# Merge gates in block products over three walks, second half normalised by way of DRAM, SSM data in fewer DMAs

## The chip, the cores and the metric

The kernel runs on one core of one Trainium2 chip. Its engines work side by side: TensorE (PE in the profile; its weight loads are PEld), VectorE (DVE), ScalarE (ACT), GpSimd (POOL) and SyncE (SP), which here issues DMAs only. The metric is the device time of one execution in microseconds. Before the change it is 2546.79 us, the median of three runs from 2544.15 to 2549.72.

## What is computed

A decoder layer on x of 1024 positions by 2048 channels, all in float32:

```
h = rms_norm(x, norm_w)
q, k, v, a_gate, u, z, g_a, g_s = split(h @ w_in)       # 1024,256,256,1024,1024,1024,2048,2048 columns
q, k = rms_norm per head of 64
y_a = (window-128 attention with sinks(q, k, v) * silu(a_gate)) @ w_attn_proj
y   = gelu(diagonal complex SSM(u))                     # 64 groups of 16 channels, 64 states each
glu_a, glu_b = split(y @ w_glu + b_glu)
y_s = (glu_a * sigmoid(glu_b) * silu(z)) @ w_ssm_proj
out = x + (sigmoid(g_a) * y_a + sigmoid(g_s) * y_s) @ w_out
```

## The kernel before

Activations lie transposed: channels on the 128 partitions, positions along the row, in two halves of 512 positions (h = 0 and 1). A float32 operand is split in two float32r tiles, hi (a cast on ScalarE) and lo (the rest, a subtraction on VectorE; `split`, L80), and a product of a 128x128 weight block with a 128x512 operand takes three matmuls: hi*hi, hi*lo, lo*hi. `proj` (L110) makes one output tile of 128 columns for one half: two weight tiles of 128x1024 (8 blocks of 128x128 each), each loaded by SyncE (`load_w`, L99: tag raw, two tiles; tags whi and wlo, two each), split, and followed by 16 hi and 8 lo matmuls; it yields behind each of the two. So an output tile of the input projection costs 48 matmuls.

The stages follow one another in the code: u and z of half 0 beside the preparation of the SSM (`ssm_prep`), k, v, q of half 0 (`kvq`), then half 1 (`build_raw(1)`, u, k, v, q) beside the attention of half 0, z and eight merge-gate tiles of half 1 beside the attention of half 1, then the other gates beside the SSM (`ssm`, L660): eight merge-gate tiles of w_in 36 to 51 (g_a), the attention gate (28 to 35) and 16 tiles of 52 to 67 (g_s) of half 1, and after `build_raw(0)`, which loads and splits x of half 0 again, the same gates of half 0. The gates' tiles go to DRAM (GD, GSD, AGD). Operands are x times norm_w alone; rstd of each position is multiplied onto the output (`sigmoids` L171, `gate` L180, `evac` L278, `uproj` L195).

The GLU and the two branch projections (`four`, L881) and the output projection (`out1` to `out3`) already use a scheme of seven block products for a 2x2 by 2x2 product: sums of weight tiles are made on GpSimd (`wadd`, L854, into tiles of tag ws), sums of operands by `combos` (L811), and the seven operands are loaded and split by `load_ops` (L779). `out2` (L1055) is the one closest to the change: for each j it loads three weight tiles (`rring`), makes two sums, two splits (`wsplit`, with a third whi/wlo pair from pool cb in `wring`) and two block products of 24 matmuls, 6 and 5.

The SSM reads its coefficients (PWD, L687, eight DMAs for each tile of eight groups), its kernel matrix (KD, L744, eight DMAs for a tile) and writes its result (YD, L760, 16 DMAs for a tile) on SyncE's queue; px (L703) and py (L752, L753) are its matmuls, bm and ct the tables that GpSimd makes for them (tt, L665).

What runs when is decided at build time. Side work is a generator that `drive` pulls at a given rate for each step of the main one (`spawn`, L1122); a scheduler then puts the instructions of each engine in one fixed order by priority (weights are lifted by `high_priority`), and takes tile buffers from the pools as they come free. On the chip each engine goes through its order and waits at each instruction for what it needs.

## Time and profile before

| | us |
|---|---|
| median of three runs | 2546.79 |
| the profiled execution | 2542.53 |
| its span, first to last instruction | 2540.8 |
| TensorE busy | 2459.2 (97%) |
| VectorE busy | 1557.5 (61%) |
| ScalarE busy | 963.8 (38%) |
| GpSimd busy | 921.5 (36%) |
| mean granted clock of TensorE | 0.988 of 2.4 GHz |

The rows further down come from this one execution. Busy TensorE time is the union of overlapping matmuls, so the rate of matmuls is read from where they start. A row of DMA issues counts the issues of one line and says how long after its issue a transfer has landed.

### The profile page before, as it was taken

The numbers are of one execution on the slowest core, as the hardware profiler recorded it, in microseconds if no ns is written. First come the engines' busy times: TensorE is split into PE (matmuls) and PEld (weight loads), VectorE is DVE, ScalarE is ACT, GpSimd is POOL, SyncE is SP. The second block draws the span as 40 slices with busy tenths as digits, with TensorE's granted clock in tenths as the row PEclk, the third lists the DMA queues.
The fourth block names the chain that finished last, engine by engine and source line by source line (L and its number), as shares of the span: only waits on it lengthen the run. The fifth ranks groups of instructions, "written<-read, shape, count | busy, mean of one in ns | idle before, by whom it ended". The sixth has DMA issues, their size and how long they took to land. (4 is left out here: it accounts for less than half of the span.)

```text
span 2540.8 us, 30817 instructions
## 1 busy us (share of the span) xinstructions
PE 2459.2 (97%) x11012; PEld 2007.1 (79%) x11012; DVE 1557.5 (61%) x2040; ACT 963.8 (38%) x1492; POOL 921.5 (36%) x715
## 2 busy tenths in 40 slices
PE   7999999999999999999999999999999999899998
PEld 5878878788878878888788788887878877678886
DVE  7995566894686455736573432236587687745543
ACT  5333454463666433434442222224352331333311
POOL 5101004341453434251412300014547466414576
PEclk9999999999999999999999999999999999999999
DMA  6544343323223456565757743336368676888675
GB/s 212 177 135 133 92 141 104 96 72 99 96 92 121 141 161 165 177 166 142 206 159 240 259 164 124 120 120 216 108 223 296 203 252 227 266 298 278 222 234 176
DMA packets 217306, 438.95 MB, mean 173 GB/s; under 512 B 63521, under 2 KB 75841, under 8 KB 217153
## 3 DMA queue, kind: packets, MB, share of 16 engines
q1 hardware_dynamic: 181376, 344.34, 44.4%
q0 software_dynamic: 19504, 63.28, 6.6%
q10 hardware_dynamic: 16272, 29.38, 3.0%
q8 instruction: 86, 1.41, 0.2%
q14 instruction: 68, 0.55, 0.1%
HBM read 341.93 MB, written 94.96 MB: 172 GB/s over the span
## 5 line engine op out<-in xcount | busy, mean ns | idle before, releaser
L121 PE MATMUL ps<-hh,whi 128*128 128x512 f32 x2144 | 845.3, 395 | 4.7 <-ACT whi L81 4.7
L122 PE MATMUL ps<-hl,whi 128*128 128x512 f32 x2144 | 842.1, 393 | 1.0 <-DVE hl L144 1.0
L82 DVE TENSOR_TENSOR wlo<-wraw,whi 128x1024 fp32r<-128x1024 f32 (+1 forms) x344 | 445.2, 1295 | 488.9 <-PE ps L125 247.7
L81 ACT CAST whi<-wraw 128x1024 fp32r<-128x1024 f32 (+1 forms) x344 | 349.8, 1018 | 637.2 <-PE ps L122 372.0
L125 PE MATMUL ps<-hh,wlo 128*128 128x512 f32 x2144 | 542.0, 391 | 1.7 <-DVE wlo L82 1.7
L121 PEld LDWEIGHTS ps<-hh,whi 128*128 128x128 f32 x2144 | 405.1, 189 | 93.8 <-ACT whi L81 6.4
L122 PEld LDWEIGHTS ps<-hl,whi 128*128 128x128 f32 x2144 | 405.3, 189 | 86.7 <-DVE hl L144 2.1
L125 PEld LDWEIGHTS ps<-hh,wlo 128*128 128x128 f32 x2144 | 401.5, 188 | 86.9 <-DVE wlo L82 2.1
L81 ACT CAST whi<-ws 128x1024 fp32r<-128x1024 f32 x80 | 84.2, 1054 | 292.5 <-POOL ws L855 80.4
L82 DVE TENSOR_TENSOR wlo<-ws,whi 128x1024 fp32r<-128x1024 f32 x80 | 116.4, 1456 | 115.7 <-ACT whi L81 74.4
L855 POOL TENSOR_TENSOR ws<-wraw 128x512 f32<-128x512 f32 (+1 forms) x72 | 135.0, 1875 | 132.9 <-DVE wlo L82 95.8
L421 POOL TENSOR_TENSOR pa<-ph,c_mct 128x512 fp32r<-128x512 f32 x32 | 43.7, 1364 | 253.3 <-ACT ph L81 253.2
L178 POOL DMA_DIRECT2D gsd<-sg x32 | 17.8, 556 | 226.7 <-ACT sg L177 214.8
L177 ACT ACTIVATE sg<-sg 128x512 f32<-128x512 f32 x64 | 40.6, 634 | 136.5 <-DVE sg L176 136.4
L402 ACT ACTIVATE scs<-scs,m,rq 128x128 f32<-128x128 f32 x128 | 62.2, 487 | 61.9 <-DVE m L396 61.8
L1000 POOL TENSOR_TENSOR mt<-mt,pa 128x512 f32<-128x512 f32 x32 | 56.3, 1762 | 74.9 <-DMA sgs<-gsd 22.6
L178 POOL DMA_DIRECT2D gd<-sg x32 | 17.7, 555 | 177.7 <-ACT sg L177 165.3
L861 PE MATMUL psm<-q1h,whi 128*128 128x512 f32 x160 | 64.7, 405 | 6.8 <-ACT whi L81 6.8
L861 PE MATMUL psm<-q4h,whi 128*128 128x512 f32 x160 | 66.2, 414 | 3.0 <-DVE mt L995 3.0
L862 PE MATMUL psm<-q4l,whi 128*128 128x512 f32 x160 | 65.6, 410 | 1.4 <-DVE q4l L82 1.4
L861 PE MATMUL psm<-q2h,whi 128*128 128x512 f32 x160 | 62.7, 393 | 2.7 <-ACT qa L892 2.6
L862 PE MATMUL psn<-q3l,whi 128*128 128x512 f32 x160 | 62.8, 393 | 1.6 <-DVE q3l L82 1.6
(352 smaller groups left out, 4165.7 us busy)
## 6 DMA issues: line engine op xcount, KB each, us to landing
wraw<-w_in SPq DMA_DIRECT2D x268, 512.0 KB, 3.6
wraw<-w_out SPq DMA_DIRECT2D x72, 512.0 KB, 5.2
x<-xT SPq DMA_DIRECT2D x96, 256.0 KB, 3.9
gd<-sg POOLq DMA_DIRECT2D x32, 256.0 KB, 3.7
gsd<-sg POOLq DMA_DIRECT2D x32, 256.0 KB, 2.9
wraw<-w_glu SPq DMA_DIRECT2D x16, 512.0 KB, 4.2
wraw<-w_attn SPq DMA_DIRECT2D x16, 512.0 KB, 4.7
sga<-gd SPq DMA_DIRECT2D x32, 256.0 KB, 4.4
```

What stands on the lines that cost most here:

```text
L81: S.copy(hi, src)
L82: V.tensor_tensor(lo, src if src2 is None else src2, hi.bitcast(F32), op=ALU.subtract)
L121: PE.matmul(ps, hi[:, kk, :], rh[kt], start=(kt == 0), stop=False)
L122: PE.matmul(ps, hi[:, kk, :], rl[kt], start=False, stop=False)
L125: PE.matmul(ps, lo[:, kk, :], rh[kt], start=False, stop=(kt == last))
L177: S.activation(sg, sg, AF.Sigmoid)
L402: S.activation(sc[:, r, :], sc[:, r, :], AF.Exp, bias=m4[:, r:r + 1], scale=RQ[h, p][:, b, 2 * r + e:2 * r + e + 1], accum_out=den[:, r:r ...
L421: G.tensor_tensor(a, ph.bitcast(F32), mb, op=ALU.mult)
L855: G.tensor_tensor(o, a, b, op=ADD)
L861: PE.matmul(ps, hi[:, c0 + k, :], rh, start=(first and k == 0), stop=False, skip_group_check=True)
L862: PE.matmul(ps, hi[:, c0 + k, :], rl, start=False, stop=False, skip_group_check=True)
L1000: G.tensor_tensor(t, t, p, op=ADD)
```

## The change

The 32 merge-gate tiles of the two halves are no longer made one by one. They form 16 pairs (a tile j and the tile j + 8 of the same gate); a pair is a 2x2 product, two output tiles and two halves of positions over two halves of channels, and is made with seven block products instead of eight, in three walks over the pairs:

- `gates1`: products 1 and 2 with the plain operands of half 1 give one of the four outputs; product 1 is kept in DRAM (QG[0]).
- `gates2`: three weight tiles, two sums on GpSimd in place (in the raw tiles), products 6 and 5; two intermediate results go to DRAM (QG[1], QG[2]).
- `gates3`: four weight tiles, three sums, products 7, 4 and 3, which give the other three outputs.

`inputs` makes the operand sums (HD) and the normalised operands of half 1 (HN), from x blocks loaded through GpSimd's queue, while k, v, q and the attention gate of half 0 are made; `build_n` reads half 1 back from HN, so that no rstd is multiplied onto the outputs of half 1. `build_raw(0)` is gone. Attention gates are plain tiles: of half 0 ahead of the attention (kept in AT and multiplied onto it in `combos`), of half 1 beside the SSM. The SSM's coefficients are written 16 times over in DRAM and read in one DMA, its matrix is first laid out in DRAM (TZD) and read in one DMA, its result is written in two DMAs by ScalarE's queue; YD's layout and the order of w_glu's rows follow. Weights have three raw tiles in pool w, and one instead of two in pool cb, which exists from the seventh pair of the third walk on; pool g has 8 buffers and holds operands 6 and 7, pool g2 four more.

```diff
+RAW = 3
...
-    YD = dp.tile([2, NG * 16, 8, 64], F32, name="yd")
-    PWD = dp.tile([2, 8, NG, 64], F32, name="pwd")
+    YD = dp.tile([2, 8, 128, 8, 64], F32, name="yd")
+    PWD = dp.tile([2, 8, 16, NG, 64], F32, name="pwd")
...
-        raw = wp.tile([128, KC, 128], F32, tag="raw", name="wraw")
+        raw = wp.tile([128, KC, 128], F32, tag="raw", bufs=RAW, name="wraw")
...
-    def build_raw(h):
+    def build_n():
...
-            x = load_x(kt, h, tag="ld" if kt % 2 else "x")
+            x = sp.tile([128, TH], F32, tag="ld" if kt % 2 else "x", bufs=3 if kt % 2 else 2, name="hn")
+            nc.sync.dma_start(x, HN[kt])
...
     def evac(ps, out, h):
-        V.tensor_tensor(out, ps, rstd[h], op=ALU.mult)
+        if h:
+            S.copy(out, ps)
+        else:
+            V.tensor_tensor(out, ps, rstd[h], op=ALU.mult)
...
-                    for j in range(8):
-                        nc.sync.dma_start(w[n][16 * j:16 * j + 16],
-                                          PWD[n, 7 - j, g0:g0 + 8, :].unsqueeze(0).to_broadcast([16, 8, 64]))
+                    nc.sync.dma_start(w[n], PWD[n, :, :, g0:g0 + 8, :].rearrange("j h g p -> (j h) g p"))
...
-                for j in range(8):
-                    nc.sync.dma_start(tz[16 * j:16 * j + 16],
-                                      KD[:, gs + q * 8:gs + q * 8 + 8, 128 - 16 * j:256 - 16 * j])
+                nc.sync.dma_start(tz, TZD[:, gs + q * 8:gs + q * 8 + 8, :])
...
-                for i in range(8):
-                    for s in range(2):
-                        nc.sync.dma_start(YD[s, g0 * 16:(g0 + 8) * 16, i, :].rearrange("(g h) c -> h g c", h=16),
-                                          yt[16 * i:16 * i + 16, :, 64 * s:64 * s + 64])
+                for s in range(2):
+                    nc.scalar.dma_start(YD[s, 2 * bt + q], yt[:, :, 64 * s:64 * s + 64])
...
+        for k in range(8):
+            b12, b11 = block(k, 0, "x"), block(k, 1, "x")
+            nc.gpsimd.dma_start(HN[k], b11)
+            G.tensor_tensor(b11, b11, b12, op=SUB)
+            nc.gpsimd.dma_start(HD[0, k], b11)
+            yield
...
+    def gates1(ops, a, b):
+        for p in range(a, b):
+            kind, _, na, nb, ia, ib = PAIRS[p]
+            with tc.high_priority(offset=200):
+                t1 = wsplit(rring(wq(na, 0)))
+            x = bank(0)
+            product(x, t1, 0, ops[1])
+            q = et("qa")
+            S.copy(q, x)
+            nc.gpsimd.dma_start(QG[0][p], q)
+            yield
...
+            product(x, t2, 0, ops[2], first=False)
+            gate(kind, ia, 1, x)
+            yield
+
+    def gates2(ops, a, b):
+        for p in range(a, b):
+            kind, _, na, nb, ia, ib = PAIRS[p]
+            q = ld(QG[0][p], "qa")
+            with tc.high_priority(offset=200):
+                w5, r, w6 = rring(wq(nb, 0)), rring(wq(nb, 1)), rring(wq(na, 0))
+                wadd(w5, w5, r)
+                wadd(w6, w6, w5)
+                t = wsplit(w6)
+            y = bank(0)
+            product(y, t, 0, ops[6])
+            v = et("qb")
+            V.tensor_tensor(v, q, y, op=SUB)
+            nc.gpsimd.dma_start(QG[1][p], v)
+            yield
+            with tc.high_priority(offset=200):
+                t = wsplit(w5)
+            y = bank(0)
+            product(y, t, 0, ops[5])
+            e = et("qe")
+            V.tensor_tensor(e, y, v, op=ADD)
+            nc.gpsimd.dma_start(QG[2][p], e)
+            yield
...
+                    w[7], r, w[4], w[3] = rring(wq(na, 0)), rring(wq(nb, 0)), rring(wq(nb, 1)), rring(wq(na, 1))
+                    wadd(w[7], w[7], r)
...
+                    wadd(w[3], w[3], w[4])
+                    wadd(w[3], w[3], w[7])
+                    t = wsplit(w[3])
+                y = bank(1 if p > 5 else 0)
+                product(y, t, 0, ops[3])
+                gate(kind, ia, 0, y, ADD, e)
...
+            product(z, t, 0, ops[7])
+            gate(kind, ib, 0, z, SUB, e)
...
+            product(z, t, 0, ops[4], first=False)
+            gate(kind, ib, 1, z, SUB, v)
...
-    spawn(ssm(bp, pp), 0.8)
-    drive(sigmoids(36, GD[1], hh, hl, rstd[1], 8, 16))
-    drive(gate(28, AGD[1], hh, hl, rstd[1], AOD[1]))
-    drive(sigmoids(52, GSD[1], hh, hl, rstd[1], 0, 16))
-    hh, hl = build_raw(0)
-    drive(gate(28, AGD[0], hh, hl, rstd[0], AOD[0]))
-    drive(sigmoids(36, GD[0], hh, hl, rstd[0], 0, 16))
+    spawn(ssm(bp, pp), 1.1)
+    drive(plain("o", 28, 1, hh, hl))
+    drive(gates1(og, 8, 12))
+    operands((6,), 1.5)
+    drive(gates1(og, 12, 15))
...
+    operands((3,), 1.5)
+    drive(gates2(og, 0, 15))
+    drain2()
+    operands((7, 4), 4.0)
+    drive(gates2(og, 15, 16))
+    drain2()
+    drive(gates3(og, 0, 6))
     drain()
```

Where the order of instructions moves, at the places that the prediction speaks of:

GpSimd beside the SSM, before (the gate tiles of half 1; bm, bmu, ct and ctu are the SSM's tables, the DMAs the gate tiles):

```order
L665 TENSOR_TENSOR ct<-c_9116,p_8212 128x1152
L665 TENSOR_TENSOR ct<-ct,ctu 128x1152
L665 TENSOR_TENSOR ctu<-c_9945,p_9196 128x1152
L178 DMA gsd_81<-sg 128x512 x2
L665 TENSOR_TENSOR bm<-pwr,bre 128x8x64
L665 TENSOR_TENSOR bm<-pwr,bim 128x8x64
L665 TENSOR_TENSOR ct<-c_9944,p_9195 128x1152
L665 TENSOR_TENSOR bm<-bm,bmu 128x8x64
L665 TENSOR_TENSOR ct<-ct,ctu 128x1152
L665 TENSOR_TENSOR bmu<-pwi,bre 128x512
L665 TENSOR_TENSOR ctu<-c_10065,p_9196 128x1152
```

GpSimd beside the SSM in the second walk, after (L849 are the weight sums, L1199 and L1207 the DMAs of QG; the pair's second sum stands three rows further down, behind a bm and another L1199):

```order
L849 TENSOR_TENSOR wraw<-wraw 128x1024
L645 TENSOR_TENSOR bm<-pwr,bre 128x8x64
L645 TENSOR_TENSOR bm<-pwr,bim 128x8x64
L645 TENSOR_TENSOR ct<-c_10215,p_9529 128x1152
L645 TENSOR_TENSOR bm<-bm,bmu 128x8x64
L1199 DMA qg_96<-qb 128x512
L645 TENSOR_TENSOR ct<-ct,ctu 128x1152
L645 TENSOR_TENSOR bmu<-pwi,bre 128x512
L1207 DMA qg_97<-qe 128x512
L645 TENSOR_TENSOR ctu<-c_10292,p_9530 128x1152
L849 TENSOR_TENSOR wraw<-wraw 128x1024
```

The SSM's operations were alone with the gates' DMAs and stand now between weight sums on which a product waits.

SyncE in the second pass of the output projection, before, with what each issue waits for (the numbers tell tiles apart; DMAHW are earlier DMAs):

```order
L843 DMA wraw_18842<-w_out 128x1024 [waits DMAHW6_49,Pool_49]
L843 DMA wraw_18844<-w_out 128x1024 [waits DMAHW7_49,Pool_49]
L843 DMA wraw_18846<-w_out 128x1024 [waits DMAHW0_49]
L878 DMA qa_18840<-qd0_92 128x512 [waits DMAHW2_49,DVE_49]
L843 DMA wraw_18942<-w_out 128x1024 [waits DMAHW3_49,Pool_49]
L843 DMA wraw_18944<-w_out 128x1024 [waits DMAHW6_49,DMAHW5_49,Pool_49]
L843 DMA wraw_18946<-w_out 128x1024 [waits DMAHW7_49]
L878 DMA qa_18940<-qd0_92 128x512 [waits DMAHW0_49,DVE_49]
```

SyncE in the second walk, after:

```order
L837 DMA wraw_10906<-w_in 128x1024 [waits DMAHW7_49,DMAHW1_49,Pool_49]
L872 DMA qa_11021<-qg0_95 128x512 [waits DMASW3_49,DVE_49]
L837 DMA wraw_10908<-w_in 128x1024 [waits DMAHW3_49,DVE_49]
L837 DMA wraw_10910<-w_in 128x1024 [waits DMAHW4_49,DVE_49]
L837 DMA wraw_11023<-w_in 128x1024 [waits DMAHW5_49,DMAHW3_49,Pool_49]
L872 DMA qa_11129<-qg0_95 128x512 [waits DMAHW6_49,DMASW5_49,DVE_49]
L837 DMA wraw_11025<-w_in 128x1024 [waits DVE_49]
L837 DMA wraw_11027<-w_in 128x1024 [waits DMAHW0_49,DVE_49]
L837 DMA wraw_11131<-w_in 128x1024 [waits DMAHW7_49,DMAHW1_49,Pool_49]
```

A raw tile was free as soon as GpSimd had added it; now the second and third load of a pair wait for VectorE, which splits the sums out of the raw tiles.

## Rows read from the trace of the kernel before

**Rows 1.** Page, part 1: busy us (share of the span) and instructions of each engine.

```profile
PE 2459.2 (97%) x11012; PEld 2007.1 (79%) x11012; DVE 1557.5 (61%) x2040; ACT 963.8 (38%) x1492; POOL 921.5 (36%) x715
```

**Rows 2.** Windows: stretch, its us, busy PE PEld DVE ACT POOL, PEclk, DMA, GB/s.

```profile
1420.00:1710.00 290.00, 289.11 (x1262) 238.55 (x1263) 96.22 (x100) 80.75 (x95) 31.62 (x43) 0.99 0.46 152
1710.00:1745.00 35.00, 30.53 (x120) 21.38 (x120) 22.56 (x27) 14.40 (x23) 15.57 (x17) 1.00 0.77 249
...
2045.00:2225.00 180.00, 161.08 (x656) 126.62 (x655) 136.42 (x146) 45.25 (x61) 104.88 (x64) 0.95 0.74 244
...
2316.00:2403.00 87.00, 87.00 (x385) 72.03 (x385) 40.96 (x44) 21.95 (x27) 42.23 (x17) 1.00 0.78 260
```

**Rows 3.** Timeline of PE, second pass of the output projection: start us, us, instruction.

```profile
2331.01 0.39 PE L861 MATMUL psn<-q6h,whi 128*128 128x512 f32 x1
...
2336.45 0.39 PE L861 MATMUL psn<-q5h,whi 128*128 128x512 f32 x1
...
2352.77 0.39 PE L861 MATMUL psn<-q6h,whi 128*128 128x512 f32 x1
...
```

**Rows 4.** Lines by form, GpSimd: x count | busy us, mean ns | idle before.

```profile
L855 POOL TENSOR_TENSOR ws<-wraw 128x1024 f32<-128x1024 f32 x24 | 60.0, 2499 | 57.0 <-DVE wlo L82 27.5 <-DMA wraw<-w_out 10.3 <-DMA x<-xT 5.0
...
L665 POOL TENSOR_TENSOR bm<-bm,bmu 128x512 f32<-128x512 f32 x16 | 26.4, 1650 | 0.3
...
L665 POOL TENSOR_TENSOR ct<-ct,ctu 128x1152 f32<-128x1152 f32 x8 | 24.6, 3073 | 0.3
...
L665 POOL TENSOR_TENSOR ctu<-c,p 128x1152 f32<-128x1152 f32 x8 | 21.2, 2652 | 0.2
...
L178 POOL DMA_DIRECT2D gsd<-sg x32 | 17.8, 556 | 226.7 <-ACT sg L177 214.8 <-ACT X L735 8.6 <-DMA pwi<-pwd 3.3
...
```

**Rows 5.** Timeline of GpSimd in the SSM; last row: PE's px, lines by form.

```profile
890.99 2.27 POOL L665 TENSOR_TENSOR ctu<-c,p 128x1152 f32<-128x1152 f32 x1
893.22 1.29 POOL L665 TENSOR_TENSOR bm<-bm,bmu 128x512 f32<-128x512 f32 x1
...
895.06 2.68 POOL L665 TENSOR_TENSOR ct<-ct,ctu 128x1152 f32<-128x1152 f32 x1
...
L703 PE MATMUL px<-uq,bm 128*128 128x128 f32 x128 | 18.5, 306 | 9.3 <-POOL bm L665 9.3
```

**Rows 6.** DMA issues of SSM data: x count, KB each, median us to landing.

```profile
tz<-kd SPq DMA_DIRECT2D x64, 64.0 KB, 3.5
...
yd<-yt SPq DMA_DIRECT2D x128, 32.0 KB, 2.7
...
pwr<-pwd SPq DMA_DIRECT2D x64, 32.0 KB, 2.1
...
```

**Rows 7.** Timeline of the output projection's second pass: sums, splits, casts, an issue.

```profile
2327.97 3.31 POOL L855 TENSOR_TENSOR ws<-wraw 128x1024 f32<-128x1024 f32 x1 [4.97 <-DMA x<-xT]
...
2334.86 1.23 DVE L82 TENSOR_TENSOR wlo<-ws,whi 128x1024 fp32r<-128x1024 f32 x1 [5.24 <-ACT whi L81]
...
2339.78 2.39 POOL L855 TENSOR_TENSOR ws<-wraw,ws 128x1024 f32<-128x1024 f32 x1 [1.21 <-DVE wlo L82]
...
2342.20 1.06 ACT L81 CAST whi<-ws 128x1024 fp32r<-128x1024 f32 x1 [4.00 <-POOL ws L855]
...
2351.38 0.33 SPq L843 DMA_DIRECT2D wraw<-w_out  x1
```

**Rows 8.** DMA issues of weights, with median us to landing.

```profile
wraw<-w_in SPq DMA_DIRECT2D x268, 512.0 KB, 3.6
wraw<-w_out SPq DMA_DIRECT2D x72, 512.0 KB, 5.2
```

**Rows 9.** Waits of GpSimd: combos behind VectorE; us in total, times, longest.

```profile
POOL cb_b L820 <- DVE cb_d L819: 48.3, 11, 10.2
```

**Rows 10.** Lines by form: a split of operand tiles on VectorE.

```profile
L82 DVE TENSOR_TENSOR q7l<-op,q7h 128x512 fp32r<-128x512 f32 x20 | 18.9, 996 | 5.8 <-ACT q7h L81 5.6
```

**Rows 11.** Tile ws (sums of weights): ns at least, in the middle, at most.

```profile
L82 DVE TENSOR_TENSOR wlo<-ws,whi x80: 1207/1225/3981, 1706.2 to 2513.9; 128x1024 fp32r<-128x1024 f32 x80
```

241 lines of the change are left out of this document (168 added, 73 removed).

## Prediction

> **What bounds the kernel now.** I read the shares of the engines first: TensorE is busy in 2459.2 of 2540.8 us [rows 1], so the kernel can gain in two ways only, fewer matmuls or fewer of the 82 us in which TensorE stands. Next come the stretches [rows 2]. The one that the change rewrites most (gate projections, 1420 to 1710) has TensorE busy in 289.11 of 290 us at a granted clock of 0.99: no wait is left to win there. TensorE stands elsewhere, 4.5 us at the start of the GLU (1710 to 1745) and 19 us in the last branch product (2045 to 2225). The rate of TensorE is read off a timeline [rows 3]: 24 matmuls start between 2331.01 and 2336.45 us, so a block product of 24 takes 5.44 us and a matmul 0.2267 us.
>
> **What the change takes off TensorE.** The order of instructions has 10,050 matmuls of 128x512 before and 9,666 after: the 32 merge-gate tiles in two halves cost 32 x 2 x 48 = 3,072, the 16 pairs cost 16 x 7 x 24 = 2,688. 384 x 0.2267 = **87.1 us**, all on the path, since TensorE has no idle time in that stretch to swallow it [rows 2].
>
> **What it adds beside TensorE.** GpSimd gets 80 sums of weight tiles (128x1024; two a pair in the second walk, three in the third), 2.50 us in the mean [rows 4] and mostly 2.39; 40 differences and sums of input tiles; and the DMA issues of HD, HN and QG, 0.556 us each. ScalarE and VectorE split 16 weight tiles fewer and 40 operand tiles more. None of this is on TensorE's path by itself; what counts is how far ahead of TensorE a weight is ready. I take the stages in order.
>
> *Inputs (beside k, v, q and the attention gate of half 0).* 40 tile operations of 1.29 to 1.65 us and 88 issues of 0.556 us are 101 to 115 us of GpSimd [rows 4, 5]. Cover: 20 tiles x 10.9 = 218 us of TensorE's work. If it fails, the second half's operands come late: up to 10 us. I take 0.
>
> *SSM data in few DMAs.* 320 issues on SyncE (64 and 64 of PWD, 64 of KD, 128 of YD [rows 6]) become 24 there and 16 on ScalarE. TensorE's px matmuls wait 9.3 us in all, and for GpSimd's bm [rows 5], which stays; so 0.
>
> *Normalising once.* 16 tiles read back from DRAM replace two times 16 of x, and VectorE loses its scale by rstd in half 1. TensorE doesn't wait for either today: 0.
>
> *First walk.* One load and one split for each block product, as before: 0.
>
> *Second walk, the tight one.* A pair needs three loads, two sums on GpSimd and two splits, and TensorE gives it 10.88 us. The same pattern runs today in the second pass of the output projection, with TensorE busy in all 87 us [rows 2]. There the sums have tiles of their own and a third hi/lo pair exists: by the order of sums and casts, the sum that ends at 2342.17 us is for the product that begins at 2352.77, ten us of cover [rows 3, 7]. The change has three raw tiles, sums in place, and two hi/lo pairs. By its order the third load of a pair waits for VectorE's split of the previous pair's w5; that split waits for a lo tile which TensorE frees at the start of the previous pair's product 6. From there: split 1.23 us, issue 0.33, landing, sum 2.39, cast 1.05 [rows 7]. With the landing of w_out, 5.2 us, that is 10.2 us; with that of w_in, 3.6 us, 8.6 us [rows 8]. I take the slower as nearer, since the output pass loads the same three tiles a step. So the ring has 0.7 to 2.3 us of cover in 10.88.
>
> Now GpSimd's queue. At two places nine instructions of the SSM and of QG stand between the last sum of one pair and the first of the next, and two more before the second. From last sum to last sum that is 20.2 us with the short rows (1.29 for a bm or bmu, 2.27 for a ct or ctu, 2.68 for their sum, 0.56 for an issue, 2.39 for a weight sum [rows 5, 7]) and 23.3 with the means (1.65, 2.65, 3.07, 0.56, 2.50 [rows 4]). TensorE has 10.88 us plus half a px block, 18.5/16 = 1.2 us [rows 5]: 12.1. It stands 20.2 - 12.1 - 2.3 = 5.8 to 23.3 - 12.1 - 0.7 = 10.5 us; I take 8, twice: 16. The pair behind each burst has 11.8 to 13.8 us of GpSimd: 0.7 each. The other 12 pairs can slip by 0 to 1 us; I take 0.3, since their cover is positive. **Second walk: 21 us** (12 to 36).
>
> *Into the third walk.* Its first product needs three sums. Behind the second burst GpSimd has six bm or bmu, three issues and these sums, 16.6 to 19.1 us; TensorE has 12.1. 4.5 to 7, I take **5**.
>
> *Third walk, pairs 0 to 5* (three raw tiles, four loads): a sum frees a tile, a load fills it (0.33 and landing), two sums, another load, a sum: 15.0 us with 3.6 to land, 18.2 with 5.2, against 16.3 of TensorE. Middle 16.6: 0.3 x 6 = **2** (0 to 11).
>
> *Third walk, pairs 6 to 15.* A fourth raw tile and a third hi/lo pair exist, but eight combos share GpSimd: three sums, three gate issues, two operations and four issues of a combo are 13.7 to 15.3 us in 16.3. Its queue also stops when a combo's tiles are late, 48.3 us in 11 waits today [rows 9], now with weight sums behind: 13.7 + 4.4 would be 1.8 over in eight pairs, 14; 15.3 + 4.4 would be 27; never late 0. I take **6** (0 to 27).
>
> *GLU start.* Before, 12 of its 28 operand tiles go into free tiles ahead of time and 16 come late. Now all but two wait for tiles of the gate operands: ten more at 1.0 us of VectorE each [rows 10], begun 5.44 us earlier: **5** (0 to 10).
>
> **Sum.** 2542.5 (the profiled execution: span 2540.8 and 1.7 around it) - 87.1 + 21 + 5 + 2 + 6 + 5 = 2494.4. The median of the runs before is 4.3 above that execution; with it **2498.7 us**, said as 2499. With all low ends (12 + 4.5) it is 2476, with all high ends (36 + 7 + 11 + 27 + 10, and 10 for the inputs) 2561.
>
> **A rule weighed.** Do VectorE's splits and GpSimd's sums stop each other? The rows have the split at 1207 ns at the least, 1225 in the middle, 3981 at most [rows 11], and one sum at 3.31 us [rows 7]. The Trainium skill (SBUF — State Buffer, Who interferes with whom) says that a VectorE instruction with two SBUF inputs and a GpSimd instruction that reads SBUF exclude each other, the second one blocked until the first is done. By that rule a split could lose a whole sum, 2.4 us, in each pair of the second walk, 1.7 past its cover of 0.7, 27 us more in 16 pairs; by the rows the middle split loses nothing. At its worst it is rival 3.
>
> **Rivals.**
> 1. *The cover holds* (20%). The bursts find GpSimd ahead and operands come in time, 12 us of costs in all: 2542.5 - 87.1 + 12 + 4.3 = 2472. For it: the output pass runs this pattern with no loss [rows 2]. Against: its extra tiles.
> 2. *The ring has no cover* (13%). Landings are slower beside SSM and QG traffic; each pair of the second walk slips 2 us and each of the third 1 us more, 48 us on top of the forecast: 2547, no change.
> 3. *Slower: splits and sums hold each other up* (8%). In the second walk, with 3.98 for the split, 3.31 for a sum and 5.2 to land, the ring takes 13.9 us against 10.88: 42 us in 14 pairs. The two bursts (23.3, and 0.8 more for each of two sums, less 12.1) cost 26, the way into the third walk 9. Pairs 0 to 5 of the third take 21.0 against 16.3: 28; the others carry 17.7 of GpSimd against 16.3: 14. Together 119: 2542.5 - 87.1 + 119 + 4.3 = 2579. It is slower than before from 87 us of such loss on. For it: 3.98 and 3.31 occur [rows 7, 11]. Against: the medians.
> 4. *The change doesn't do what it says*: the count of matmuls excludes that for TensorE; for the SSM's DMAs it may hold, and costs nothing.
>
> **How the numbers follow.** Forecast 54%, nearly all of it faster; rival 1 20%; rival 2 13%, split evenly over faster, same and slower; rival 3 8%; 5% for a stall that I don't see, half of it slower. 0.2% of the time is 5 us, about what a measurement of this kernel can tell from no change. Faster 0.81, same 0.07, slower 0.12. Eight in ten: from 2466, a little below rival 1, to 2540, which leaves out rival 3 and most of rival 2.
>
> **What would show it.** Right: 9,666 wide matmuls at 0.227 us; TensorE's idle time grows by some 40 us; in the second walk (about 190 us with the SSM's matmuls) two waits of 6 to 10 us stand where ScalarE's cast waits for a GpSimd sum and TensorE for the cast. Wrong on the low side: TensorE over 97% busy in that walk. Wrong on the high side: most pairs of it wait for a cast or a split, or the sums and splits are near 3 us in the mean. A wait of TensorE on SSM data, or a gap at the first projection of half 1, would contradict my zeros.

## Result and the profile of the changed kernel

The changed kernel takes 2575.55 us (median of 4 runs, 2572.14 to 2575.95), the kernel before 2548.26 beside it: 1.0103 times as long (95% interval 1.0080 to 1.0125): 27 us by these medians, 1.0% slower. The prediction was 2499 and its range ended at 2540. It was wrong in sign and in size.

Page of the changed kernel, part 1, which answers to [rows 1]:

```profile
PE 2404.5 (93%) x10628; PEld 1955.8 (76%) x10628; DVE 1671.7 (65%) x2052; ACT 958.0 (37%) x1528; POOL 1253.6 (49%) x1001
```

The 384 matmuls are gone (11,012 before). But TensorE's busy time fell by 54.7 us, not by 87.1: the matmuls that are left take 32.4 us more. And TensorE stands 168.9 of 2573.4 us, where it stood 81.6 of 2540.8: 87.3 more. -87.1 + 32.4 + 87.3 = +32.6, the difference of the two spans. So everything that the block products saved was given back as waits, and more than a third as much again as slower matmuls.

Where: windows of the changed kernel, the first, second and third walk, and everything from the GLU on (columns as in [rows 2]):

```profile
839.00:1152.00 313.00, 301.86 (x1417) 248.76 (x1416) 196.41 (x225) 153.45 (x269) 151.49 (x125) 1.00 0.56 173
1152.00:1410.00 258.00, 213.10 (x965) 175.59 (x964) 163.33 (x174) 73.07 (x122) 164.91 (x102) 0.93 0.67 210
1410.00:1742.00 332.00, 286.83 (x1187) 230.38 (x1188) 177.98 (x175) 101.80 (x142) 190.04 (x151) 0.93 0.75 242
1742.00:2573.00 831.00, 786.49 (x3387) 639.33 (x3385) 526.73 (x563) 253.91 (x341) 436.71 (x297) 0.98 0.69 229
```

The second and third walk stand out: TensorE idle for 45 us in each, and a granted clock of 0.93, where the gate stretch of [rows 2] had 0.99. GpSimd works 355 us of these 590. From the GLU on it is 831 us against 828.5 before (2540.8 - 1712.3), so next to nothing was lost there.

What TensorE waits for in the two walks (us in total, times, longest):

```profile
PE psm L855 <- ACT whi L88: 33.4, 12, 5.6
PE psm L855 <- DVE gx L1145: 23.2, 10, 6.2
PE py L728 <- DMA tz<-tzd: 13.8, 3, 8.3
PE px L681 <- POOL bm L645: 8.1, 3, 3.8
PE psn L858 <- DVE wlo L89: 5.4, 2, 3.1
```

No single wait leads. Weights come late (whi), the gates that have to read a bank before product 4 can go on in it come late (gx), and SSM's data come late (tz, bm). A timeline shows one such wait of the third walk from its root (start us, us, instruction):

```profile
1581.61 5.71 DVE L89 TENSOR_TENSOR wlo<-wraw,whi 128x1024 fp32r<-128x1024 f32 x1 [1.79 <-ACT whi L88]
...
1582.03 1.30 POOL L813 TENSOR_TENSOR cb_b<-cb_b 128x512 f32<-128x512 f32 x1
...
1583.84 2.39 POOL L849 TENSOR_TENSOR wraw<-wraw 128x1024 f32<-128x1024 f32 x1
...
1587.24 0.68 DVE L1145 TENSOR_TENSOR gx<-psn,qe 128x512 f32<-128x512 f32 x1
...
1589.05 0.68 DVE L1145 TENSOR_TENSOR gx<-psm,qe 128x512 f32<-128x512 f32 x1
...
1589.87 0.77 PE L855 MATMUL psm<-q4h,whi 128*128 128x512 f32 x1 [2.62 <-DVE gx L1145]
...
1590.86 0.63 PE L855 MATMUL psm<-q4h,whi 128*128 128x512 f32 x1
...
```

A split of a weight tile, 1.225 us in the middle, takes 5.71 us here, and ends only after GpSimd's sum (1583.84 + 2.39 = 1586.23). The first gate queued behind it on VectorE is 4.4 us late. The second, whose bank is complete at 1587.26 us, starts only at 1589.05, behind two combo operations that the split held up as well; TensorE stands 2.62 us for it, and the next matmuls run at the lower clock (0.63 us in the row, where 0.39 is usual; the granted clock from 1589.8 to 1592.6 is 0.50).

Who is stretched: the split and the gate by tile, in the two walks (ns at least, in the middle, at most), and two of the SSM's step operations by line:

```profile
L89 DVE TENSOR_TENSOR wlo<-wraw,whi x80: 1208/1225/5706, 1156.1 to 1739.2; 128x1024 fp32r<-128x1024 f32 x80
...
L1145 DVE TENSOR_TENSOR gx<-psm,qe x22: 674/682/692, 1424.3 to 1741.4; 128x512 f32<-128x512 f32 x22
L1145 DVE TENSOR_TENSOR gx<-psm,qb x15: 676/683/692, 1444.7 to 1727.5; 128x512 f32<-128x512 f32 x15
L1145 DVE TENSOR_TENSOR gx<-psn,qe x9: 676/679/692, 1564.5 to 1731.8; 128x512 f32<-128x512 f32 x9
...
L645 DVE TENSOR_TENSOR v<-v,v x33: 293/424/3282, 1155.3 to 1471.2; 128x256 f32<-128x256 f32 x15, 128x896 f32<-128x896 f32 x6, 128x240 f32<-128x240 f32 x3, 128x224 f32<-128x224 f32 x3
L645 DVE TENSOR_TENSOR X<-X,v x22: 409/426/2636, 1151.9 to 1472.3; 128x256 f32<-128x256 f32 x16, 128x896 f32<-128x896 f32 x6
```

Splits and SSM steps read two SBUF tiles and are stretched, by up to 4.5 us, which is several GpSimd instructions in a row. The gates read one PSUM bank and one SBUF tile and are never stretched (692 ns at most). That is the rule of the Trainium skill (SBUF — State Buffer, Who interferes with whom) that rival 3 of the prediction was built on: a VectorE instruction with two SBUF inputs and a GpSimd instruction that reads SBUF exclude each other, one with a single SBUF input, outside VectorE's 2-port modes, does not. These rows agree with it. So does the timeline of the two walks: 25 of the 80 splits took over 1.4 us, and each of the 25 ends 1.08 to 1.10 us after the end of a GpSimd operation on SBUF tiles. One thing differs from the rule as the prediction tells it, the second one blocked until the first is done: three of the 25 lost two or three such GpSimd operations in a row, and the split shown above had begun 0.42 us before the first of them. That the rule sets the time had still to be shown.

### The profile page after: what moved, and what is told of

It reads as the page before. It is cut to its first block, busy times and chain, and to the rows that moved or that the text cites. A ratio compares the mean times of both kernels' runs of the same rounds, so it can differ in the third digit from the quotient of the medians.

```text
span 2573.4 us, 30421 instructions
## 1 busy us (share of the span) xinstructions
PE 2404.5 (93%) x10628; PEld 1955.8 (76%) x10628; DVE 1671.7 (65%) x2052; ACT 958.0 (37%) x1528; POOL 1253.6 (49%) x1001
## 5 line engine op out<-in xcount | busy, mean ns | idle before, releaser
L128 PE MATMUL ps<-hh,whi 128*128 128x512 f32 x1120 | 444.5, 397 | 0.4 <-ACT whi L88 0.4
L129 PE MATMUL ps<-hl,whi 128*128 128x512 f32 x1120 | 442.4, 395 | 0.0
L132 PE MATMUL ps<-hh,wlo 128*128 128x512 f32 x1120 | 285.1, 392 | 0.4 <-DVE wlo L89 0.4
L849 POOL TENSOR_TENSOR wraw<-wraw 128x1024 f32<-128x1024 f32 x80 | 197.3, 2467 | 153.6 <-DMA wraw<-w_in 142.0
L128 PEld LDWEIGHTS ps<-hh,whi 128*128 128x128 f32 x1120 | 213.0, 190 | 48.8 <-issue 1.5
L129 PEld LDWEIGHTS ps<-hl,whi 128*128 128x128 f32 x1120 | 212.9, 190 | 44.8 <-issue 0.5
L132 PEld LDWEIGHTS ps<-hh,wlo 128*128 128x128 f32 x1120 | 209.4, 188 | 45.2 <-DVE wlo L89 0.9
L849 POOL TENSOR_TENSOR ws<-wraw 128x512 f32<-128x512 f32 (+1 forms) x72 | 135.9, 1888 | 164.8 <-DVE wlo L89 122.7
L855 PE MATMUL psm<-q7h,whi 128*128 128x512 f32 x288 | 114.5, 398 | 6.2 <-ACT whi L88 6.2
L856 PE MATMUL psm<-q7l,whi 128*128 128x512 f32 x288 | 113.9, 395 | 0.0
L855 PE MATMUL psm<-hh,whi 128*128 128x512 f32 x256 | 100.8, 394 | 4.4 <-ACT qa L1177 3.2
```

The costliest lines, as they stand in the source:

```text
L128: PE.matmul(ps, hi[:, kk, :], rh[kt], start=(kt == 0), stop=False)
L129: PE.matmul(ps, hi[:, kk, :], rl[kt], start=False, stop=False)
L132: PE.matmul(ps, lo[:, kk, :], rh[kt], start=False, stop=(kt == last))
L849: G.tensor_tensor(o, a, b, op=ADD)
L855: PE.matmul(ps, hi[:, c0 + k, :], rh, start=(first and k == 0), stop=False, skip_group_check=True)
L856: PE.matmul(ps, hi[:, c0 + k, :], rl, start=False, stop=False, skip_group_check=True)
```

## The experiments

All ratios are to the kernel before, run beside each kernel on the same chip; the changed kernel has 1.0103. A gain "in us" of a single edit is the difference of two ratios, times 2549 us.

**Four first edits: bank, ring, engine, SSM.** The waits above suggest a cause each. `bank4` takes away the wait for gx:

```diff
+            v = ld(QG[1][p], "qb")
+            V.tensor_tensor(v, z, v, op=SUB)
             yield
...
-            product(z, t, 0, ops[4], first=False)
-            gate(kind, ib, 1, z, SUB, v)
+            y = bank(0)
+            product(y, t, 0, ops[4])
+            gate(kind, ib, 1, y, ADD, v)
```

> The changed kernel, but product 4 of the third walk goes into a bank of its own: z - v is formed by one more VectorE instruction (v = z - v, some 0.68 us, 16 of them), and product 4 no longer has to wait until both readers of z are done. Theory A, the bank: TensorE waits 23.2 us in the third walk for gx (10 waits, up to 6.2 us) only because product 4 accumulates on the bank that VectorE has still to read; then these waits go, and with the clock that returns the time falls by 20 to 30 us, to 2545 to 2555 us. Theory B, the ring of raw tiles: the weights of product 4 and 3 are late anyway, the wait is then shown for whi instead, and the time falls by less than 8 us (over 2567). Theory C, GpSimd beside VectorE: gx is late because the weight splits ahead of it on VectorE are stretched (5.7 us where 1.22 is usual); the bank hides up to 5 us of that, so C gives as A here, 20 to 30 us less, but the stretched splits (14 in the third walk, 25 us over the usual) stay.

Measured: 2570.59 us, ratio 1.0069 (1.0048 to 1.0089), 0.34% or 9 us less, with intervals that overlap. The wait for gx is gone, but others have taken its place; TensorE's waits in its two walks begin with

```profile
PE psm L855 <- ACT whi L88: 24.1, 14, 4.2
PE psn L855 <- ACT whi L88: 16.0, 6, 7.5
PE py L728 <- DMA tz<-tzd: 11.8, 3, 7.0
```

So the bank was where the delay showed, not where it came from: theory A falls as the main cause. Theory C had forecast 20 to 30 us here too and missed; only theory B's forecast, another wait and little gain, came near.

`ring4` gives the walks a fourth raw weight tile:

```diff
-        if cbp is not None and ring[1] % 4 == 0:
-            t = cbp.tile([128, KC, 128], F32, tag="raw", name="wraw")
+        if xp is not None and ring[1] % 4 == 0:
+            t = xp.tile([128, KC, 128], F32, tag="raw", name="wraw")
...
+    xp = ctx.enter_context(tc.tile_pool(name="xr", bufs=1))
     bp = tc.alloc_tile_pool(name="b", bufs=1)
```

> The changed kernel, but the fourth raw weight tile (4 KB per partition) that it has from pair 6 of the third walk on is there from the last quarter of the first walk. Theory B, the ring: in the second walk the third load of a pair (w6) has to wait for a tile that is free only when the split of the pair before is done; with a fourth tile it is issued about 5 us earlier, so the 20.9 us of waits for whi in the second walk (8) and 12.5 in the third shrink to under 10 together and the time falls by 20 to 35 us, to 2540 to 2555. Theory S, the queue on SyncE: the raw loads stand behind loads of qa, qb and qe, which wait for their own tiles (52 us of issue waits for gx in the third walk); a fourth tile then brings under 8 us. Theory C (GpSimd beside VectorE): the sums and splits themselves are late, under 8 us.

Measured: 2564.18 us, ratio 1.0042 (1.0025 to 1.0059), 0.6% or 16 us less, under the 20 that theory B asked for and over the 8 that theories S and C left. The waits for whi did not shrink (56.3 + 5.7 us in its two walks, 33.4 in the changed kernel). The ring of three tiles has a share, but not the main one.

`sums_v` moves the sums:

```diff
-                wadd(w5, w5, r)
-                wadd(w6, w6, w5)
+                V.tensor_tensor(w5, w5, r, op=ADD)
+                V.tensor_tensor(w6, w6, w5, op=ADD)
...
-                    wadd(w[7], w[7], r)
+                    V.tensor_tensor(w[7], w[7], r, op=ADD)
...
```

> The changed kernel, but the 80 weight sums of the second and third walk are done by VectorE in place of GpSimd. Theory C, GpSimd and VectorE in each other's way: the 24 stretched splits of these two walks (15 and 25 us over the usual length) mostly go, the sum takes 1.2 us where GpSimd took 2.39, VectorE's busy time in the two walks rises by 80 x 1.2 = 96 us to about 75% of them, and the time falls by 20 to 40 us, to 2535 to 2555. Theory B (ring): the chain of a pair gets shorter by 1.2 us for each sum but its loads come as late as before; 5 to 15 us less. Against both: VectorE takes its work in order, a sum that waits for a load holds up the splits and gates behind it (as GpSimd's sums waited 138 us for raw loads); then slower than 2575, up to 2600.

Measured: 2550.28 us, ratio 0.9988 (0.9973 to 1.0003), 1.15% or 29 us less, within theory C's range. VectorE's own queue takes part of the gain back: its sums now wait for raw tiles, 33.5 us in 12 places for the first sum of the second walk, 25.8 for that of the third.

`halfssm` leaves out batches 3 and 4 of the SSM:

```diff
+            if bt > 1:
+                for q in range(2):
+                    yt = tl((128, 8, NCH), "yt", 1)
+                    S.activation(yt, uq[:, q * 8:q * 8 + 8, :], AF.Gelu_apprx_tanh)
...
+                continue
```

> The changed kernel with batches 3 and 4 of the SSM left out (their output is replaced by the activation of their input), which takes px, py and the GpSimd bursts of bm and ct out of the second walk. TensorE loses 128 x 3 / 2 = 192 instructions of 0.275 us = 52.8 us. Theory D, SSM as the cause: the 24 us of waits of the second walk for tz, bm and X go too, and without the bursts most of the 20.9 us of whi: 2575 - 53 - 24 - 15 = about 2483, the rest of the second walk then near 174 us for its 768 wide products. Theory B (ring): only SSM's own waits go, the whi waits of the second walk stay at 20 us or grow, since nothing is left beside which they hide: 2575 - 53 - 20 = about 2500, up to 2515.

Measured: 2538.28 us, ratio 0.9942 (0.9920 to 0.9964): 41 us less though TensorE lost 52.8 us of work. Neither theory gave so little. Waits for whi are 48.2 us in its two walks: without SSM's matmuls TensorE waits more for weights. In the second walk it has 135 instructions less (830 against 965), some 37 us at 0.275 us each, and the walk is 18 us shorter (240 against 258), so there TensorE's own work sets the pace only in part. The combos also moved up into the second walk, so the run is no clean measure of the SSM.

**Is it the SSM's share of GpSimd?** `ssm_v` moves its tables to VectorE:

```diff
-                tt(bm[:, :, 0, :], w[0], w[2], mul, G)
+                tt(bm[:, :, 0, :], w[0], w[2], mul)
...
-                ct = ctable(bp, tt, G, p1, p2, gs + q * 8, 8, q * 8, 1)
+                ct = ctable(bp, tt, V, p1, p2, gs + q * 8, 8, q * 8, 1)
```

> The changed kernel with SSM's GpSimd work (bm and ct, 18 instructions of 1.3 to 3 us a batch) on VectorE; the weight sums stay on GpSimd, which then has only sums, stores and combos. Theory F, the queue of GpSimd, as the prediction has it (two bursts between the sums of the second walk, 8 us each): those two waits go, the second walk falls by 15 to 25 us to 232 to 242, the time to 2550 to 2560. Theory C (VectorE and GpSimd in each other's way) and the queue of VectorE: it has 60 to 70 us more in the two walks, splits wait behind SSM's tables, and the time falls by less than 8 us or rises.

Measured: 2552.35 us, ratio 1.0016 (1.0002 to 1.0030), 0.9% or 22 us less, as theory F said in sum but not in place: the second walk stayed (264 us, with 30 instructions of TensorE more in it), and the third fell to 302. So the two bursts of the prediction are not what holds up the second walk, unless VectorE, which then works 197 us of it in place of 163, took back what GpSimd gave. In the third walk TensorE has 59 instructions less than in the changed kernel (1128 against 1187) and VectorE 57 us less work (121 against 178), since the SSM ends before it: part of the 30 us is work that moved. How much of the rest comes from the tables stays open.

**What do the sums cost at all, and through what?** Five kernels in a row, all without the 80 sums, so that the products use the first raw tile of each. `nosum` only drops them:

```diff
-                wadd(w5, w5, r)
-                wadd(w6, w6, w5)
...
```

> The changed kernel without the 80 weight sums of the second and third walk: all loads, casts, splits and matmuls stay, the products take the first raw tile of each sum as it is loaded (the gates are then other numbers). It says how much of the 119 us that the two walks stand over their own work (47 + 10 in the second, 48 + 21 in the third as gaps and slow matmuls, and the SSM's own waits) hangs on the sums at all. Theory G, the sums on GpSimd (their place in its queue behind SSM and stores, and the splits that they stretch): nearly all of it but SSM's own 24 us goes, 2575 - 80 to 95, so 2480 to 2495. Theory B/E (loads come late, from the ring of three tiles or from DMA engines at 0.67 to 0.75 of their time): the waits move from whi <- sum to whi <- load, and less than 40 us goes, 2535 or more.

`idlesum` gives GpSimd as much work in their places, with results that nobody reads (two such lines a sum, one for each half of the raw tile):

```diff
-                wadd(w5, w5, r)
+                G.tensor_tensor(rstd[0], r[:, 0:4].rearrange("p a b -> p (a b)"), rstd[1], op=ADD)
+                G.tensor_tensor(rstd[0], r[:, 4:8].rearrange("p a b -> p (a b)"), rstd[1], op=ADD)
...
```

> The kernel without the 80 weight sums (2475 us), but GpSimd does as much work in their places: two additions of 128x512 for each sum, which read the raw tile of the sum and write into a tile that nobody reads. Casts, splits and products wait for none of them (the gates are other numbers). Theory C, exclusion: what GpSimd does costs because VectorE's instructions are stretched meanwhile (115 us over their usual length in the two walks of the changed kernel, 36 without sums, 63 with the sums on VectorE); then most of the loss is back, 2520 or more, with 80 us or more of stretch. Theory G, the chain: the loss comes from casts that wait for a sum in GpSimd's queue; then the time stays near that without sums, 2475 to 2495, though VectorE is stretched as much. If both have a share the time is between, and says the shares of the 100 us.

`tinysum` reads a sliver of the raw tile instead, `busysum` has full additions that read partial products and no raw tile, and `memsum` is tinysum with five memsets behind each sliver:

```diff
# tinysum
-                wadd(w5, w5, r)
+                G.tensor_tensor(rstd[0][:, 0:8], r[:, 0, 0:8], rstd[1][:, 0:8], op=ADD)
...
# busysum, twice for each sum
+            G.tensor_tensor(rstd[0], v, rstd[1], op=ADD)
...
# memsum, five times behind each line of tinysum
+                G.memset(rstd[0], 0.0)
...
```

> The kernel without the 80 weight sums, with one tiny GpSimd instruction (128x8) in the place of each, which reads the raw tile of the sum and writes where nobody reads (the gates are other numbers). The raw tile still comes free only when GpSimd has come to it in its queue, but the sums' 200 us of GpSimd time are gone. Theory R, the ring through GpSimd's queue: most of the 100 us stays, 2540 or more. Theory C, GpSimd's busy time stretches VectorE's instructions: 2475 to 2495, with 36 to 50 us of stretch in the two walks as without sums.

> The kernel without the 80 weight sums, with two additions of 128x512 on GpSimd in the place of each, which read loaded or stored partial products (v and e), never a raw weight tile, and write where nobody reads. GpSimd's time is as with the sums, the raw tiles come free as without them. Theory C: 2540 or more, with 80 us or more of stretch on VectorE in the two walks. Theory R: 2475 to 2500 in spite of the stretch. If this and tinysum both come out near 2520 both have a share; if both are near 2480 it takes the two together.

> The kernel with the tiny GpSimd instruction in place of each sum (tinysum, 2478 us), each followed by five memsets of 128x512 on GpSimd, about 0.45 us each by the one memset in the trace (1.794 us for 2048 columns), 2.3 us a sum: GpSimd's queue is as full as with the sums, but what fills it reads nothing from SBUF. Theory P, VectorE's two-operand instructions and GpSimd's exclude each other: memsets do not stretch VectorE, so the time stays at 2478 to 2495, with the stretch in the two walks near 35 us. Theory Q, GpSimd's queue (SSM tables, stores and combos behind the sums come late): 2540 to 2575 as with busysum and idlesum. In between: shares of both.

Measured, with the busy time of GpSimd and VectorE in the second and third walk together and the length of the two (from the windows below; those of the changed kernel are above):

| kernel | GpSimd does in place of the sums | GpSimd us | VectorE us | walks us | time us | ratio (95%) |
|---|---|---|---|---|---|---|
| nosum | nothing | 164 | 268 | 488 | 2475.37 | 0.9701 (0.9680 to 0.9721) |
| tinysum | a sliver, reads the raw tile | 184 | 264 | 493 | 2478.40 | 0.9720 (0.9703 to 0.9737) |
| memsum | the sliver and 2.7 us that read nothing | 391 | 270 | 535 | 2513.35 | 0.9857 (0.9840 to 0.9874) |
| busysum | 2.6 us that read other tiles | 375 | 374 | 549 | 2543.18 | 0.9970 (0.9956 to 0.9985) |
| idlesum | 2.6 us that read the raw tile | 381 | 361 | 592 | 2574.88 | 1.0091 (1.0073 to 1.0109) |
| changed kernel | the sums | 355 | 341 | 590 | 2575.55 | 1.0103 (1.0080 to 1.0125) |

Windows of nosum, tinysum, memsum, busysum and idlesum, second and third walk each:

```profile
1142.00:1361.00 219.00, 205.69 (x983) 171.49 (x982) 126.36 (x173) 72.52 (x120) 85.84 (x70) 0.98 0.79 244
1361.00:1630.00 269.00, 263.62 (x1191) 218.22 (x1190) 141.57 (x188) 104.79 (x148) 78.40 (x106) 1.00 0.89 297
```

```profile
1144.00:1369.00 225.00, 210.40 (x982) 174.00 (x983) 125.68 (x176) 75.60 (x125) 92.28 (x103) 0.97 0.78 241
1369.00:1637.00 268.00, 264.38 (x1192) 219.57 (x1190) 138.65 (x179) 105.00 (x146) 91.69 (x151) 0.99 0.88 296
```

```profile
1145.00:1381.00 236.00, 208.06 (x983) 172.00 (x981) 137.31 (x191) 79.33 (x134) 182.66 (x271) 0.95 0.79 242
1381.00:1680.00 299.00, 275.22 (x1189) 226.07 (x1190) 132.85 (x171) 104.50 (x144) 207.95 (x376) 0.94 0.81 263
```

```profile
1140.00:1381.00 241.00, 214.27 (x952) 175.33 (x951) 169.49 (x170) 72.10 (x121) 150.99 (x121) 0.94 0.71 217
1381.00:1689.00 308.00, 283.36 (x1248) 232.21 (x1246) 204.85 (x187) 105.91 (x151) 224.13 (x204) 0.96 0.78 258
```

```profile
1143.00:1402.00 259.00, 214.93 (x964) 174.66 (x962) 176.45 (x174) 73.40 (x122) 171.26 (x133) 0.95 0.68 212
1402.00:1735.00 333.00, 289.10 (x1209) 234.59 (x1210) 184.97 (x183) 105.86 (x149) 210.23 (x196) 0.92 0.75 240
```

Read downwards. The sums cost 100 us in all (2575.6 - 2475.4), and 102 in the two walks. Loads are not the reason: nosum loads every byte that the changed kernel loads, at 297 GB/s and 0.89 of the DMA engines' time, with TensorE busy 263.62 of 269 us. That a cast waits for a sum is not needed for the loss either: in idlesum no cast does, and all 100 us are back, so theory G falls, though nosum alone seemed to prove it (idlesum's GpSimd works 26 us more than the changed kernel's, so a small share of the chain is not excluded). That a raw tile comes free only after GpSimd has come to it costs 3 us by itself (tinysum), which the intervals do not tell from nothing. A full GpSimd queue on top of that costs 35 (memsum), with VectorE as quick as before.

The rest, 62 us from memsum to idlesum (57 in the walks), is the largest step, and it comes with reading: VectorE's busy time goes from 270 to 361 us for about the same count of instructions (362 and 357), because they wait inside themselves. That is theory C/P, the exclusion. It is not cleanly alone in these 62 us: idlesum's additions also hold the raw tile some 2.6 us longer than memsum's sliver. busysum, which reads as much but leaves the raw tiles alone, has VectorE stretched as far (374 us) and loses 68 us against nosum, but its walks are only 14 us longer than memsum's, its time 30; its additions stand at other places, behind the products. idlesum has 32 us more than busysum for the same GpSimd time: there GpSimd reads raw tiles, and the ring of three waits for it. So reading costs 14 us of the walks where it leaves the ring alone and 57 where it holds the ring's tiles. How these 57 divide between the stop and the longer hold was not tried; that a fourth tile alone gives back 16 us (ring4) speaks for the stop.

Of the forecasts, theory C's came for idlesum, tinysum and busysum, theory R's for neither of the last two, and memsum came out between P and Q.

The Trainium skill (SBUF — State Buffer, Who interferes with whom) also says that a GpSimd instruction that only writes SBUF does not contend with two-input VectorE instructions. memsum agrees: 207 us of GpSimd more than in tinysum, and VectorE at 270 against 264 us.

**One part alone: SSM data in few DMAs.** The kernel before with only that part (first with the rows of w_glu left in the old order, then in the new):

```diff
-                    for j in range(8):
-                        nc.sync.dma_start(w[n][16 * j:16 * j + 16],
-                                          PWD[n, 7 - j, g0:g0 + 8, :].unsqueeze(0).to_broadcast([16, 8, 64]))
+                    nc.sync.dma_start(w[n], PWD[n, :, :, g0:g0 + 8, :].rearrange("j h g p -> (j h) g p"))
...
-                for j in range(8):
-                    nc.sync.dma_start(tz[16 * j:16 * j + 16],
-                                      KD[:, gs + q * 8:gs + q * 8 + 8, 128 - 16 * j:256 - 16 * j])
+                nc.sync.dma_start(tz, TZD[:, gs + q * 8:gs + q * 8 + 8, :])
...
```

> The kernel before with one part of the change alone: SSM data in few DMAs (PWD written 16 times over and read by one DMA each, TZD read by one DMA in place of eight, the result stored by two DMAs of ScalarE's queue in place of 16 of SyncE's). The prediction has 0 for it: within 4 us of the kernel before. Theory D, the one large load of tz comes later than eight small ones (13.8 us of waits for tz in the changed kernel, none in the kernel before): 5 to 15 us slower, with waits of py for tz. Against it, the 30 issues fewer per half batch on SyncE let the weights go earlier: 3 to 8 us faster.

> Again the kernel before with the SSM data in few DMAs alone, now with the rows of w_glu in the order that the new layout of the SSM's result needs (in the run before_ssm they were in the old order, so that the GLU computed other numbers; no instruction differs). All theories: 0.9909 of the kernel before again, within 0.2%, 20 to 26 us less.

Measured: 2527.88 us, ratio 0.9909 (0.9894 to 0.9924), and 2523.84 us, 0.9891 (0.9873 to 0.9909): 23 to 28 us less, far beyond every expectation. The SSM's stretch of the kernel before and of before_ssm2, windows:

```profile
880.00:1450.00 570.00, 553.58 (x2598) 461.83 (x2596) 318.82 (x417) 222.43 (x328) 194.82 (x149) 0.99 0.62 185
```

```profile
880.00:1450.00 570.00, 567.42 (x2688) 474.65 (x2687) 331.51 (x428) 226.43 (x335) 190.53 (x156) 1.00 0.64 195
```

In the same 570 us TensorE gets 90 more instructions done and stands 2.6 us in place of 16.4. What GpSimd waited for in the kernel before, same stretch:

```profile
POOL bm L665 <- DMA bre<-sBrT: 11.4, 2, 6.5
...
POOL bm L665 <- DMA c<-sC: 9.1, 1, 9.1
...
POOL bm L665 <- DMA bim<-sBiT: 5.5, 1, 5.5
```

None of the three is in this window of before_ssm2, but the first has only moved. GpSimd's first bm of the SSM waits for its loads there too, and starts 6.2 us earlier than in the kernel before; first the row before, then that of before_ssm2, then TensorE's wait for bm that is left of the 9.3 us:

```profile
883.27 2.06 POOL L665 TENSOR_TENSOR bm<-pwr,bre 128x512 f32<-128x512 f32 x1 [9.13 <-DMA c<-sC]
```

```profile
877.05 1.28 POOL L670 TENSOR_TENSOR bm<-pwr,bre 128x512 f32<-128x512 f32 x1 [13.60 <-DMA bre<-sBrT]
```

```profile
PE px L706 <- POOL bm L670: 1.5, 1, 1.5
```

So GpSimd's bm, for which TensorE's px waits [rows 5], was itself waiting for loads that stood behind 16 small issues of PWD on SyncE (868.32 to 879.14 us, the load of bre at 879.19). That is 8 of the 14 us. The other 6 are a stall of the kernel before around 1410 to 1420 us, which before_ssm2 has not. There VectorE and ScalarE wait for loads of YD; a weight split and a weight cast stand behind these two, and TensorE behind them:

```profile
1412.20 0.69 DVE L819 TENSOR_TENSOR cb_d<-cb_b 128x512 f32<-128x512 f32 x1 [7.13 <-DMA cb_b<-yd]
...
1418.80 0.62 ACT L81 CAST q1h<-op 128x512 fp32r<-128x512 f32 x1 [11.84 <-DMA op<-yd]
```

Which piece of the edit removed that stall was not tried. Over the whole run TensorE stands 9.4 us less and its matmuls take 8.5 us less (2450.7 against 2459.2). tz from one large load costs nothing there, so theory D falls; why the changed kernel waits for it (13.8 us, 9.2 without the sums) stays open.

**A kernel that beats both.** `best3` puts sums_v, ring4 and bank4 together; `best4` also makes the attention's combos during the GLU; `best5` has the sums of the branch and output products on VectorE as well.

> The three edits together: sums on VectorE (-29 us measured alone), a fourth raw tile from the first walk on (-16), a bank of its own for product 4 (-9). If the three act on separate waits they add: 2575 - 54 = about 2521, 1.2% below the kernel before. If all three shorten one and the same chain (load, sum, cast, split) the sum is not much better than the best of them: 2540 to 2550, no change against the kernel before. I expect between, 2530 to 2540.

Measured: 2513.03 us, ratio 0.9842 (0.9821 to 0.9863), 62 us under the changed kernel by the medians, no less than the 54 of the three alone (the difference is within the intervals). So the three waits were not one chain. The second walk is down to 215 us. The largest wait left stands at the start of the GLU (1640 to 1700):

```profile
PE psm L855 <- ACT q1h L88: 23.8, 4, 11.5
```

```diff
-    spawn(combos(Ba, CBD["a"], 4, AT), 0.4)
     drive(gates3(og, 11, 15))
...
+    spawn(combos(Ba, CBD["a"], 4, AT), 0.2)
     stage(glu, oy, load_ops(oa, source(Ba, CBD["a"]), 4, ORDER))
```

> The three edits of best3 (2513 us), and the combos of the attention's operands made during the GLU in place of the end of the third walk. In best3 TensorE stands 24 us at the start of the GLU for q1h, whose loads stand behind those combos in SyncE's queue and wait for their tiles. Theory: that wait goes, 2485 to 2500. Rival: the loads of the GLU's operands are late for another reason (their tiles are freed by the last combos of y, or the gate operands hold them), then no change; or the combos stretch the GLU instead, which has four sums a product pair on GpSimd, then 2513 to 2530.

Measured: 2508.13 us, ratio 0.9830 (0.9815 to 0.9846), which the intervals do not tell from best3. That wait is gone and the third walk is 11 us shorter (296 against 307), but from the GLU on it takes 851 us against 847 in best3, though those had the wait in them: the combos now share GpSimd and VectorE with the GLU's sums. Mostly the rival.

```diff
     def wadd(o, a, b):
-        G.tensor_tensor(o, a, b, op=ADD)
+        V.tensor_tensor(o, a, b, op=ADD)
```

> best4 (2508 us) with the 112 weight sums of the branch and output products on VectorE too, not only the 80 of the gates. In best4 TensorE waits 21 us for wlo from the GLU on, in 13 places, and 64 us of gaps and 24 us of slow matmuls stand there. Theory C (GpSimd's sums stretch the splits of wlo): 20 to 40 us less, 2470 to 2490. Against it: VectorE is busy in 587 of these 851 us already, the sums add some 100 us, and what waits in its queue is then late for that; no change or 10 to 20 us slower.

Measured: 2487.24 us, ratio 0.9763 (0.9743 to 0.9783), 2.4% faster than the kernel before. VectorE's queue did not eat the gain. From the GLU on, best4 and then best5 (windows):

```profile
1656.00:2507.00 851.00, 791.62 (x3364) 640.32 (x3362) 554.92 (x571) 250.78 (x338) 459.47 (x327) 0.97 0.72 238
```

```profile
1651.00:2492.00 841.00, 788.99 (x3363) 641.50 (x3361) 595.94 (x680) 251.64 (x338) 267.80 (x218) 0.97 0.73 240
```

VectorE takes 109 instructions and 41 us more, GpSimd 192 us less, and the stretch is 10 us shorter. The other half of the 21 us between the two medians cannot be placed from one profile of each.

## Why the prediction was wrong, step by step

- *Matmuls, -87.1.* Right in count (384). Wrong in what it leaves out: a matmul's price depends on the clock, which was 0.93 in the two walks. The working had no term for the 32 us that the remaining matmuls got dearer.
- *Inputs, 0 (up to 10).* At the bad end: TensorE now waits for k and v beside them, 7.5 us of the 10 (rows of the changed kernel, 150 to 300 us; before_ssm2, without that work, has 1.0 us there):

```profile
PE pvt L299 <- DVE vn L255: 4.7, 1, 4.7
PE pk L276 <- ACT sqh L88: 2.8, 1, 2.8
```

- *SSM data, 0.* The step that failed is "for GpSimd's bm [rows 5], which stays": it took the releaser in the profile as the end of the chain and did not ask what GpSimd waited for. The part is worth 23 to 28 us in the kernel before; if it is worth as much in the changed one, which no run shows, it hid as much of the loss elsewhere.
- *Normalising once, 0, and first walk, 0.* Nearly right: the clock in the first walk is 1.00, and of the 11 us in which TensorE stands there 4.3 are the walk's own (3.2 for the copy of product 1, 1.1 for whi).
- *Second walk, 21 (12 to 36), into the third 5, third walk 8 (0 to 38).* Together 34; by the windows with and without sums (258 against 219, 332 against 269) they cost 39 and 63. The failed step is the way the sums were priced: as 2.39 us of GpSimd's time and a place in a chain of load, sum, cast, split. The chain can be cut and the time stays (idlesum against the changed kernel). What costs most, 57 us from memsum to idlesum, is GpSimd's reading, by which a sum stops VectorE's two-input instructions, and with them whatever is queued behind in order: gates, splits, SSM steps, then casts, tiles, loads (with the longer hold of the raw tiles in it). Some 42 are the full queue itself (memsum against tinysum), of which the working had the tables and the combos, but not at this size.
- *A sum of the working.* The 15.3 us for the pairs 6 to 15 come to 14.7 with the means that it names elsewhere (2.50 three times, 1.65 twice, 0.556 seven times); the term's high end is then 22 in place of 27, and rival 3 is 113 in place of 119. The forecast does not change.
- *GLU start, 5 (0 to 10).* The stretch from the GLU on is 2.4 us longer; no wait of TensorE over 0.8 us stands in its first 58 us.
- *The bursts, 8 us twice.* Not found: taking them off GpSimd left the second walk as long as it was (VectorE then has 34 us more work there, which may hide a gain).
- *The rule weighed.* It was the right rule, with the wrong row: [rows 11] shows splits from stages that hold none of the SSM's steps, and the working took their median. I charged the rule to the splits alone, once a pair. The walks also hold the SSM's steps, 0.42 us in the middle and up to 3.28, and the gates behind them. The row that would have told stands in the trace of the kernel before, for the splits beside the SSM (870 to 1450 us), and its median is as blind as that of rows 11; the largest value is not:

```profile
L82 DVE TENSOR_TENSOR wlo<-wraw,whi x94: 1210/1224/7817, 870.8 to 1449.5; 128x1024 fp32r<-128x1024 f32 x94
```

- *Rivals.* Rival 1 (2472) is near what the kernel does without sums, 2475. Rival 3, the splits and sums that hold each other up, gave 2579 at 8% and named the cause. That it hit to 3 us is luck: it took 3.98 us for every split and 3.31 for every sum, and they took 1.73 and 2.47 in the mean, with medians of 1.225 and 2.39:

```profile
L89 DVE TENSOR_TENSOR wlo<-wraw,whi 128x1024 fp32r<-128x1024 f32 x80 | 137.8, 1730 | 98.5 <-ACT whi L88 67.4 <-PE psm L858 31.0
```

```profile
L849 POOL TENSOR_TENSOR wraw<-wraw 128x1024 f32<-128x1024 f32 x80 | 197.3, 2467 | 153.6 <-DMA wraw<-w_in 142.0
```

Its 119 us stand against 100 for the sums, 36 for waits that remain without them (nosum against the kernel before less 87.1 and 25.5), and -25 from the SSM, 111 in all. Its chance should have been several times larger, since it had a rule and the rows that showed it at work (3.98 and 3.31).
- *What would show it.* "A wait of TensorE on SSM data" came (tz, 13.8 us). "Most pairs of it wait for a cast or a split" came by half: 8 waits for whi in the 16 pairs of the second walk. Sums and splits "near 3 us in the mean" did not come. The loss is spread over more kinds of waits than the marks had: gates, SSM data and the clock as well.

## What to carry to other kernels

GpSimd was not a free engine here beside a busy VectorE: its work that reads SBUF was paid again on VectorE, in the two-input instructions that met it and in all that was queued behind. Price such work by the mean and the largest value of VectorE's two-input instructions in such a stretch, not by their median. A wait in the profile names the last link only; before a wait is counted as staying or going, follow its releaser's own wait once more. To learn what a step costs, leave it out, then put its time back without its result: here that took away the explanation that the first run alone seemed to prove.
